# One-hot tiles of the expert gate matrix: a token's columns four bytes apart instead of sixteen

## The chip, the core and the metric

The kernel runs on one core of one Trainium2 chip. The metric is the device time of one execution in microseconds (us), the median of several runs. The engines have short names in the profile: PE is TensorE's matmul and PEld its weight load, DVE is VectorE, ACT is ScalarE, POOL is GpSimd and SP is SyncE, which here only issues DMAs.

## The reference, cut to what matters

The reference is three transformer blocks, one after the other, on 256 tokens of width 1024, in float32. The change lies in the last part of the first block, a layer of 16384 one-neuron experts. Each token has 8 heads. Each head scores 128 + 128 sub-keys, retrieves the 16 best pairs of them, and weighs the 16 experts that those pairs name by a softmax:

```python
v1, i1 = lax.top_k(s1, PEER_TOPK)            # s1, s2: scores of 128 sub-keys each
v2, i2 = lax.top_k(s2, PEER_TOPK)
cand = (v1[..., :, None] + v2[..., None, :]).reshape(T, PEER_HEADS, PEER_TOPK * PEER_TOPK)
cand_idx = (i1[..., :, None] * PEER_NKEYS + i2[..., None, :])...
vals, pos = lax.top_k(cand, PEER_TOPK)
experts = jnp.take_along_axis(cand_idx, pos, axis=-1)
gates = jax.nn.softmax(vals, axis=-1)
...
u = expert_u[ec]
a = jnp.einsum('cd,chkd->chk', xc, u)
w = jax.nn.gelu(a) * gc
return jnp.einsum('chk,chkd->cd', w, expert_v[ec])
```

So a token has 8 x 16 = 128 retrieved experts. Each is named by two numbers below 128, and each has a gate.

## The kernel before

The kernel does not gather experts. It multiplies every expert with every token, and weighs the products by a gate matrix that is zero where an expert was not retrieved. Three pieces of the class `Peer` matter here.

**The gate matrix** (the last loop of `routing`, lines 878 to 902). For one token the 128 x 128 matrix of gates is a product of two one-hot matrices: entry (b, a) is the sum, over the 128 retrieved experts on the partitions, of B[expert, b] times A[expert, a]. B has a one where b is the expert's second number. E has a one where a is its first number, and A is E times the gate. The gate goes in two float16 parts, so there are two tiles A, and each token takes two matmuls that accumulate in one float32 product. The loop makes 8 tokens in a step, and there are 32 steps. In each step DVE makes E (line 888), B (line 889) and the two A (line 892), each a float16 tile of 1024 elements per partition. PE then does 16 matmuls of 128 columns (line 897), each with its own weight load, into two PSUM tiles of four tokens. ACT copies each PSUM tile into `gt` (line 900), and after every second step it issues a DMA of `gt` to a scratch tensor `gd` in DRAM (line 902).

The tiles E, B and A are laid out as [128 partitions, 128 values, 8 tokens]. One token's 128 columns, which a matmul reads as `B[:, :, token]` and `A[j][:, :, token]`, thus stand eight float16 elements apart, which is 16 bytes. All four tiles come out of one pool of eight buffers (tag `oh`), so DVE can be about two steps ahead of PE. An A of a later step takes a buffer that the matmuls of an earlier step must have left.

**The up products** (`up`, lines 904 to 914). The experts' input weights stream through SBUF in 64 chunks of 1 MB. For each chunk ACT makes the high part `wh` (line 99), and for the first 29 chunks POOL, not DVE, makes the low part `wl = raw - wh` (line 101), in two halves each. PE multiplies the chunk with all tokens by 48 matmuls of 256 columns (lines 117 to 119, output `tp`), and ACT applies gelu (line 912) and leaves the result in a buffer `ga`.

**The order.** `run` weaves the two: `weave(self.routing(), up, n)` emits the steps of `routing`, and after some of them one chunk of `up`. Thirteen chunks come among the steps ahead of the gate loop, eleven more among the first of the 32 gate steps. A scheduler then spreads the matmuls of a chunk among the gate steps, and sets one fixed order for each engine, which the engine keeps. After the loop `down` (line 916) reads the gates back from `gd`, does the chunks that are left, and multiplies with the experts' output weights.

The constant `iota` (line 772) holds the numbers 0 to 127, each eight times. It is an operand of lines 888 and 889, and its first 16 values are an operand of line 859, ahead of the gate loop.

Of the kernel before, what the change touches and what calls it, by code (L numbers as in the profile page):

```python
# [26 lines left out]
class Core:  # L27
    """Pools and the pieces that every block uses.

    Weights stream through SBUF in chunks of [128, 2048]; each float32 chunk is split  # L30
    exactly into a part with 12 significant bits and the rest, and a float32 product is
    hi*hi + hi*lo + lo*hi, accumulated in float32.
    """
# [18 lines left out]
    def ring(self, ctx, n):  # L52
        """Buffers of the weight stream, n of the split parts."""
        self.raw = ctx.enter_context(self.tc.tile_pool(name="raw", bufs=3))
        self.slots, self.turn, self.early = [], 0, []
        self.more(ctx, n)

    def more(self, ctx, n):
        """n more buffers of the split parts while ctx is open."""
        pool = ctx.enter_context(self.tc.tile_pool(name=f"split{len(self.slots)}", bufs=n))  # L60
        self.slots += [pool] * n

        def less():
            del self.slots[-n:]
        ctx.callback(less)

    def work(self, ctx, half_rows=1):
        """Buffers of the norms: rows of gains, a token tile's rows."""
        self.row_bufs = {D: 3, 512: half_rows}
        self.wk = ctx.enter_context(self.tc.tile_pool(name="wk", bufs=1))  # L70

    def temp(self, ctx, name):
        """Buffers of one part of the kernel."""
        self.tmp = ctx.enter_context(self.tc.tile_pool(name=name, bufs=2))
        return self.tmp
# [45 lines left out]
    def row(self, name, n=D, src=None, pool=None, tag=None, p=128):  # L121
        """A row of a parameter on every partition."""
        src = self.a[name] if src is None else src
        t = (pool or self.wk).tile([128, n], F32, tag=tag or f"row{n}", name="row", bufs=1 if pool else self.row_bufs.get(n, 2))[:p]
        self.nc.scalar.dma_start(t, bass.AP(tensor=src.tensor, offset=src.offset, ap=[[0, p], [1, n]]))
        return t

    def rsqrt_n(self, ss, n, m, p=128):
        """(ss / n + EPS) ** -0.5 for [p, m]."""
        nc = self.nc  # L130
        v = self.sm.tile([128, 8], F32, tag="qv", name="qv")[:p, :m]
        y = self.sm.tile([128, 8], F32, tag="qy", name="qy")[:p, :m]
        nc.gpsimd.tensor_scalar(v, ss, 1.0 / n, EPS, op0=OP.mult, op1=OP.add)
        nc.gpsimd.tensor_tensor(y, v, self.half[:p, :m], op=OP.pow)
        return y

    def rstd(self, parts, n, p=128):
        """Reciprocal root mean square of rows of n that come in one or two parts [p, m <= 512]."""
# [17 lines left out]
    def pre_norm(self, t, g):  # L156
        """xh, xl[:, :, t] = split(transpose(rmsnorm(X[t]) * g))"""
# [10 lines left out]
    def put_off(self, f, *args):  # L168
        """Emits f(*args), now or at the next flush."""
# [10 lines left out]
    def post_norm(self, t, acc, g, scale, gn=None):  # L180
        """X[t] += scale * rmsnorm(acc) * g, and the next part's pre_norm if it has gains gn."""
# [10 lines left out]
    def residual(self, t, acc, gn):  # L192
        """X[t] += acc, and the next part's pre_norm."""
# [5 lines left out]
    def to_T(self, xn, hi, lo, t, nb, kb0=0, scale=None):  # L199
        """hi, lo[:, kb0.., t] = split(transpose(xn) * scale), scale a power of two."""  # L200
# [15 lines left out]
    def cols_steps(self, w, done):  # L216
        """w: [groups, 2, 128, 4 * N], N <= 512 output columns a group; done(j, t, psum).
        The first two groups go one token tile at a time, as the tiles get ready, if the ring has room."""
# [24 lines left out]
    def linear_stat(self, hl, i, ps):  # L243
        """ps [128, n] = 128 output features by tokens; hl: a chunk [128, 2, 8, 128], i: which half."""
# [5 lines left out]
    def lead(self, ch, done):  # L250
        """Products of the chunks ch one token tile at a time, as the tiles get ready, with the tokens as
        rows; done(c, t, psum [128, 2, 128])."""
# [9 lines left out]
    def pair(self, hl, between=lambda: None):  # L262
        """The two products of a chunk."""
# [6 lines left out]
    def stat_pairs(self, chunk, n, lead=0, row=None):  # L270
        """The two products of each of n chunks. The first chunks go one token tile at a time, with the
        tokens as rows [128, 256] in row(c, t), and are then transposed."""
# [30 lines left out]
    def linear_rows(self, w, hi, lo, done, tail=3, pool=0):  # L303
        """w: [K / 256, 128, 2048] rows in pairs of blocks; hi, lo: [128, K / 128, S]."""
# [34 lines left out]
def weave(main, side, n):  # L339
    """Emits the steps of main, and n[i] steps of side after step i."""  # L340
# [5 lines left out]
def head_norm(k, pool, ps, nh, gain, tag, p=128):  # L346
    """Per-head rmsnorm of ps [p, nh * 64]; returns [p, nh, 64] in SBUF."""
# [13 lines left out]
def rope(k, pool, q, nh, cs, sn, p=128):  # L361
    """Rotary embedding of the first 16 dims of q [p, nh, 64], in place; cs, sn: [p, 16]."""
# [10 lines left out]
def attend(k, pool, p, q, segs, v, identb, sink=None):  # L373
    """Masked attention of p queries and 8 heads.

    q(h): [64, p]; segs(h): (keys [64, n], n, additive mask [p, n] or None) for each piece of the
    keys; v(s, h): [n, 64]. Returns psum [p, 8, 64] before the division, and the factors [p, 8].
    """
# [65 lines left out]
def gelu_small(k, pool, out, x, n, p):  # L444
    """tanh form of gelu for small SBUF tiles, in the table of exp."""
# [10 lines left out]
class Block1:  # L456
# [108 lines left out]
    def compress(self):  # L565
        """The compressed keys and values; yields where the tensor engine would wait."""
# [59 lines left out]
    def cmp_scores(self, t):  # L626
        """Exponentials of the compressed keys' scores [128, 8, 15] and their factors [128, 8]."""
# [21 lines left out]
    def cmp_out(self, s):  # L649
        """psum [128, 8, 64]: the exponentials' products with the compressed values."""  # L650
# [12 lines left out]
    def attention(self, t):  # L663
# [10 lines left out]
        def add(b, o, r, first=False):  # L674
            """y = or += the gated output of branch b"""
# [20 lines left out]
    def flush(self, keep=0):  # L696
        """Emits the transposes that were put off, but for the last."""
# [3 lines left out]
    def merge(self):  # L701
        k, nc, pool = self.k, self.k.nc, self.pool
        M = [k.xn() for t in range(2)]
        for h in range(2):
            ch = [k.stream(k.a["w_up_" + n][h, 0]) for n in "ab"]
            for t in range(2):
                ts = slice(t * 128, t * 128 + 128)
                c = slice(h * 512, h * 512 + 512)
                for i, n in enumerate("ab"):
# [6 lines left out]
                    # sigmoid(z) = (1 + tanh(z / 2)) / 2; the half is in to_T  # L716
# [38 lines left out]
class Peer:  # L755
    """Every expert's product with every token; a gate matrix, zero where the expert was not
    retrieved, weighs them. The gates come from the top-k of the sub-keys' scores; as two float16 parts
    of SCALE times them they keep float32's 24 bits."""
# [10 lines left out]
    def consts(self):  # L769
        k = self.k  # L770
        tl = lambda n, sh, dt=F32: self.rp.tile(sh, dt, name=n)
        self.iota = tl("iota", [128, 128, 8], F16)
        k.nc.gpsimd.iota(self.iota, pattern=[[1, 128], [0, 8]], base=0, channel_multiplier=0,
# [17 lines left out]
    def routing(self):  # L791
# [21 lines left out]
        for t in range(2):  # L813
# [40 lines left out]
            for j in range(2):  # L854
# [5 lines left out]
                                        self.iota[:, 0:16, None, :].to_broadcast([128, 16, 16, 8]), op=OP.is_equal)  # L860
# [17 lines left out]
        for t in range(2):  # L878
            n = self.GRP
            for q in range(128 // n):  # L880
                c = slice(t * 128 + q * n, t * 128 + q * n + n)
                gt = pool.tile([128, 128, n], F32, tag="g8", name="gt", bufs=2)
                for w in range(n // 8):
                    c = slice(t * 128 + q * n + w * 8, t * 128 + q * n + w * 8 + 8)
                    oh = lambda n_: pool.tile([128, 128, 8], F16, tag="oh", name=n_, bufs=8)
                    B, E = oh("B"), oh("E")
                    bc = lambda x: x[:, None, c].to_broadcast([128, 128, 8])
                    nc.vector.tensor_tensor(E, bc(self.iT[0]), self.iota, op=OP.is_equal)
                    nc.vector.tensor_tensor(B, bc(self.iT[1]), self.iota, op=OP.is_equal)
# [3 lines left out]
                    for z in range(2):  # L893
                        ps = k.tp(tag="tp")
                        for i in range(4):
                            for j in range(2):
                                nc.tensor.matmul(ps[:, i, :], B[:, :, z * 4 + i], A[j][:, :, z * 4 + i],
# [86 lines left out]
class Block2:  # L984
    def __init__(self, k, wc):
        """wc: pool of the block's constants."""
# [22 lines left out]
    def ffn(self, l, f, gn):  # L1009
        k, nc = self.k, self.k.nc  # L1010
        with ExitStack() as ctx:
# [6 lines left out]
            def hidden(x, n):  # L1018
                """The gated rows or columns of the products x [128, 2, n]."""
# [26 lines left out]
    def conv(self):  # L1046
        k, nc, a = self.k, self.k.nc, self.k.a
        with ExitStack() as ctx:
# [11 lines left out]
            # the taps: blocks 0..4 on the vector engine, 5 on ACT and GpSimd, 6 and 7 as products with diagonals,  # L1060
            # and so the first of block 4's
# [15 lines left out]
            def advance(n):  # L1077
                """n steps of the vector engine's blocks, in turn."""
# [79 lines left out]
    def hgrn(self):  # L1158
        k, nc, a = self.k, self.k.nc, self.k.a
        with ExitStack() as ctx:  # L1160
# [11 lines left out]
            # q, F and kk of a group of four heads; V and SG, two tiles each, follow them in their memory  # L1172
# [130 lines left out]
class Block3:  # L1303
    """Two layers over 16 meta tokens and the 256 tokens. The meta tokens follow the others in the
    transposed tiles; as stationary operand their hi and lo parts go side by side (rows 0 and 32 up)."""
# [47 lines left out]
    def meta_cols(self, mt, xx, k0, k1):  # L1353
        """The meta tokens' columns of blocks k0.. of xx [128, 2, n, SM]: hi, then lo 32 columns on."""
# [3 lines left out]
    def meta_mm(self, ps, mt, kb, wh, wl, start, stop):  # L1358
        """ps [64, n]: rows 0.. hi's products, rows 32.. lo's; their sum is the product."""
# [4 lines left out]
    def meta_sum(self, ps, n):  # L1364
        """[16, n] in SBUF from rows 0.. and 32.. of ps."""
# [17 lines left out]
    def qkv(self, l, pool, nt):  # L1383
        """Queries, keys and values of the layer."""
# [7 lines left out]
        def flush(keep=0):  # L1392
            """Emits the transposes that were put off, but for the last."""
# [41 lines left out]
    def attention(self, l, t, sink, g):  # L1435
        """Attention of token tile t, normalised, into yy[:, :, 0:4]."""
# [21 lines left out]
    def conv(self, l, nt):  # L1458
        """The gated convolution: yy[:, :, 4:8] = split(y * g), and the rows' rstd of y."""
# [55 lines left out]
    def out_part(self, chunks, operand, nt, done, before=lambda i: None):  # L1515
        """Products with chunks of rows (rows, c); operand(c): their pair of blocks, hi and lo [128, 2, 2, n]
        and the meta tokens' tile; done(t, [psum, psum]); before(i) emits what comes before chunk i."""
# [82 lines left out]
    def mlp(self, l, nt):  # L1600
        k, nc, a = self.k, self.k.nc, self.k.a
        with ExitStack() as ctx:
# [10 lines left out]
            def up(c):  # L1613
                """Blocks 2c and 2c + 1 of the hidden features."""
# [27 lines left out]
            def rows(c, t, p):  # L1642
                """The hidden rows of token tile t."""
# [58 lines left out]
def layout(i):  # L1702
    """The arrays of the launch: the inputs in the order in which the core reads them."""
# [107 lines left out]
```

## Time and profile before

| what | us |
|---|---|
| median of 3 runs | 3044.96 |
| the 3 runs | 3044.13 to 3054.55 |
| the profiled execution, first to last instruction (span) | 3048.1 |
| PE busy in the span | 2919.3 |
| gate loop, first to last matmul of line 897 and the step's end | 463.7 to 682.8 |
| the same as a length | 219.1 |

The page gives the profiled execution's own time as its span. It is 3.1 us (0.1%) over the median of the runs.

A row of a group of instructions reads: line, engine, operation, output <- inputs, shape, count, then the busy time of the group, the mean duration of one in ns, and the engine's idle time just before them with what ended it. A row of the timeline reads: start, duration, engine, line, operation, output <- inputs, shape, count, and in brackets the idle time before it and what ended that. A row of a table by windows gives for each engine its busy time and, in brackets, its instructions, and then the granted clock of TensorE as a share of full speed. A matmul's duration in these rows has its latency in it, so that durations of neighbours overlap. How fast matmuls follow each other is read from their starts.

### The profile page before, as it was taken

The page shows a single profiled execution, that of the slowest core. Times are in us where ns is not written, and L with a number is a line of the kernel's source. Part 1 is how long each engine was busy: PE and PEld are TensorE (multiplying, and loading weights), DVE is VectorE, ACT ScalarE, POOL GpSimd, SP SyncE. Part 2 cuts the span into 40 slices and gives each one's busy share as a digit, 9 for nine tenths or more (in the row PEclk, how much of TensorE's full clock was granted, in tenths as well). Part 3 has the DMA queues.
Part 4 walks back from the last instruction along what each step waited for, and adds up shares of the span by engine and source line. Part 5 has one row for each costly group of instructions (what it writes and reads, how often), then busy time and mean ns, then how long its engine had stood idle before and what let it go on. Part 6 is the DMA issues. An engine that isn't in the chain of part 4 may idle for free. (4 is left out here: it accounts for less than half of the span.)

```text
span 3048.1 us, 44684 instructions
## 1 busy us (share of the span) xinstructions
PE 2919.3 (96%) x18182; PEld 2586.9 (85%) x18182; DVE 1773.9 (58%) x2984; ACT 1367.2 (45%) x2318; POOL 421.3 (14%) x337
## 2 busy tenths in 40 slices
PE   8999979999999999999679999999999989999999
PEld 6787978889999988898669989898997878878897
DVE  6645693437555555655966555476655555455654
ACT  4533433335444555544535444343544444444543
POOL 2000663221000000000650000032001010000100
PEclk9968988789999999999889999999999899998999
DMA  5512433339766555554325555543554424443453
GB/s 211 187 56 85 153 124 130 134 137 324 251 205 211 206 193 193 205 187 169 131 69 182 185 194 181 192 156 116 175 182 153 145 87 166 152 139 111 145 187 111
DMA packets 105982, 496.74 MB, mean 163 GB/s; under 512 B 11040, under 2 KB 44320, under 8 KB 50224
## 3 DMA queue, kind: packets, MB, share of 16 engines
q1 hardware_dynamic: 61632, 443.15, 42.1%
q10 hardware_dynamic: 44144, 50.74, 5.0%
q8 instruction: 142, 2.33, 0.3%
q14 instruction: 64, 0.52, 0.1%
HBM read 476.03 MB, written 17.83 MB: 162 GB/s over the span
## 5 line engine op out<-in xcount | busy, mean ns | idle before, releaser
L101 DVE TENSOR_TENSOR wl<-raw,wh 128x1024 fp32r<-128x1024 f32 x764 | 915.4, 1219 | 617.7 <-ACT wh L99 616.4
L99 ACT CAST wh<-raw 128x1024 fp32r<-128x1024 f32 x848 | 861.3, 1041 | 708.2 <-PE acc L118 220.5
L117 PE MATMUL tp<-xx,wh 128*128 128x256 f32 (+1 forms) x1440 | 424.2, 295 | 5.6 <-ACT ga L912 5.6
L119 PE MATMUL acc<-xx,wl 128*128 128x256 f32 x1504 | 425.1, 283 | 2.2 <-POOL wl L101 1.4
L117 PE MATMUL acc<-xx,wh 128*128 128x256 f32 x1504 | 424.6, 282 | 2.4 <-DVE hp L1093 2.4
L118 PE MATMUL acc<-xx,wh 128*128 128x256 f32 x1504 | 425.5, 283 | 0.0
L118 PE MATMUL tp<-xx,wh 128*128 128x256 f32 (+1 forms) x1440 | 421.8, 293 | 0.0
L119 PE MATMUL tp<-xx,wl 128*128 128x256 f32 (+1 forms) x1440 | 420.6, 292 | 0.8 <-POOL wl L101 0.8
L117 PEld LDWEIGHTS tp<-xx,wh 128*128 128x128 f32 x1440 | 286.7, 199 | 10.5 <-ACT ga L912 6.0
L118 PEld LDWEIGHTS tp<-xx,wh 128*128 128x128 f32 x1440 | 287.1, 199 | 3.7
L119 PEld LDWEIGHTS acc<-xx,wl 128*128 128x128 f32 x1504 | 286.9, 191 | 2.6 <-POOL wl L101 1.6
L117 PEld LDWEIGHTS acc<-xx,wh 128*128 128x128 f32 x1504 | 286.6, 191 | 2.6 <-issue 2.6
L119 PEld LDWEIGHTS tp<-xx,wl 128*128 128x128 f32 x1440 | 286.4, 199 | 1.8 <-POOL wl L101 1.0
L118 PEld LDWEIGHTS acc<-xx,wh 128*128 128x128 f32 x1504 | 284.7, 189 | 0.0
L147 POOL TENSOR_SCALAR va<-ss 128x1 f32<-128x1 f32 (+1 forms) x49 | 26.0, 531 | 1810.3 <-ACT junk L143 1628.8
L101 POOL TENSOR_TENSOR wl<-raw,wh 128x1024 fp32r<-128x1024 f32 x84 | 219.5, 2630 | 232.8 <-ACT wh L99 221.3
L117 PE MATMUL acc<-wh,xx 128*128 128x256 f32 (+2 forms) x672 | 223.3, 334 | 3.2 <-ACT xx L112 3.2
L118 PE MATMUL acc<-wl,xx 128*128 128x256 f32 (+2 forms) x672 | 219.7, 328 | 4.2 <-DVE wl L101 4.2
L119 PE MATMUL acc<-wh,xx 128*128 128x256 f32 (+2 forms) x672 | 218.7, 328 | 1.2 <-DVE xx L113 1.2
L928 PE MATMUL o<-wh,wth 128*128 128x512 f32 x512 | 200.6, 392 | 0.0
L929 PE MATMUL o<-wl,wth 128*128 128x512 f32 x512 | 200.1, 391 | 0.0
L931 PE MATMUL o<-wh,wtl 128*128 128x512 f32 x512 | 159.9, 391 | 0.0
(480 smaller groups left out, 5113.2 us busy)
## 6 DMA issues: line engine op xcount, KB each, us to landing
raw<-in_ffn_in_dram SPq DMA_DIRECT2D x88, 1024.0 KB, 4.9
raw<-in_peer_u_dram SPq DMA_DIRECT2D x64, 1024.0 KB, 4.9
raw<-in_peer_v_dram SPq DMA_DIRECT2D x64, 1024.0 KB, 4.9
raw<-in_ffn_out_dram SPq DMA_DIRECT2D x44, 1024.0 KB, 4.9
raw<-in_w_up_dram SPq DMA_DIRECT2D x32, 1024.0 KB, 4.9
raw<-in_w_down_dram SPq DMA_DIRECT2D x32, 1024.0 KB, 4.9
gd<-gt ACTq DMA_DIRECT2D x16, 1024.0 KB, 4.0
G<-gd ACTq DMA_DIRECT2D x16, 1024.0 KB, 7.0
```

The source lines that it names most:

```text
L99: nc.scalar.copy(h[:, c], r[:, c])
L101: eng.tensor_tensor(l[:, c], r[:, c], h[:, c].bitcast(F32), op=OP.subtract)
L117: mm(out, ah, bh, start=start, stop=False)
L118: mm(out, ah, bl, start=False, stop=False)
L119: mm(out, al, bh, start=False, stop=stop)
L147: nc.gpsimd.tensor_scalar(v, ss[:, 0:1], EPS, ss[:, 1:2], op0=OP.add, op1=OP.add)
L928: mm(acc[t][h], wh, vh[:, h], start=st, stop=False)
L929: mm(acc[t][h], wh, vl[:, h], start=False, stop=False)
L931: mm(acc[t][h], wl, vh[:, h], start=False, stop=sp)
```

## The change

The three kinds of one-hot tiles get the layout [128 partitions, 4 pairs of tokens, 128 values, 2 tokens]. One token's 128 columns now stand two float16 elements apart, which is four bytes, within a run of 512 bytes that a pair of tokens shares. DVE's four operations in a step keep their count, their 1024 elements per partition and their type. Their patterns differ: the operand that holds the tokens' numbers or gates is now read in rows of two elements, each row 128 times over, where it was one row of eight elements, 128 times over. The output stays one unbroken run.

The numbers 0 to 127 now stand twice each in a constant of its own, `iota2`, which is read four times over in an operation. `iota` shrinks to the 16 values that line 859 (now 862) needs.

```diff
-        self.iota = tl("iota", [128, 128, 8], F16)
-        k.nc.gpsimd.iota(self.iota, pattern=[[1, 128], [0, 8]], base=0, channel_multiplier=0,
+        self.iota = tl("iota", [128, 16, 8], F16)
+        k.nc.gpsimd.iota(self.iota, pattern=[[1, 16], [0, 8]], base=0, channel_multiplier=0,
+                         allow_small_or_imprecise_dtypes=True)
+        self.iota2 = tl("iota2", [128, 128, 2], F16)
+        k.nc.gpsimd.iota(self.iota2, pattern=[[1, 128], [0, 2]], base=0, channel_multiplier=0,
                          allow_small_or_imprecise_dtypes=True)
...
-                                        self.iota[:, 0:16, None, :].to_broadcast([128, 16, 16, 8]), op=OP.is_equal)
+                                        self.iota[:, :, None, :].to_broadcast([128, 16, 16, 8]), op=OP.is_equal)
...
-                    oh = lambda n_: pool.tile([128, 128, 8], F16, tag="oh", name=n_, bufs=8)
+                    oh = lambda n_: pool.tile([128, 4, 128, 2], F16, tag="oh", name=n_, bufs=8)
                     B, E = oh("B"), oh("E")
-                    bc = lambda x: x[:, None, c].to_broadcast([128, 128, 8])
-                    nc.vector.tensor_tensor(E, bc(self.iT[0]), self.iota, op=OP.is_equal)
-                    nc.vector.tensor_tensor(B, bc(self.iT[1]), self.iota, op=OP.is_equal)
+                    bc = lambda x: x[:, c].rearrange("p (a b) -> p a b", b=2)[:, :, None].to_broadcast([128, 4, 128, 2])
+                    iota = self.iota2[:, None].to_broadcast([128, 4, 128, 2])
+                    nc.vector.tensor_tensor(E, bc(self.iT[0]), iota, op=OP.is_equal)
+                    nc.vector.tensor_tensor(B, bc(self.iT[1]), iota, op=OP.is_equal)
                     A = [oh(f"A{j}") for j in range(2)]
                     for j in range(2):
                         nc.vector.tensor_tensor(A[j], E, bc(self.gT[j]), op=OP.mult)
...
-                                nc.tensor.matmul(ps[:, i, :], B[:, :, z * 4 + i], A[j][:, :, z * 4 + i],
+                                nc.tensor.matmul(ps[:, i, :], B[:, z * 2 + i // 2, :, i % 2], A[j][:, z * 2 + i // 2, :, i % 2],
                                                  start=j == 0, stop=j == 1)
```

On PE, DVE, ACT and SP the instructions stand in the same order as before. On POOL one instruction is added, where the experts' part begins. The rows show the difference there, with `hss`, `qv`, `va` and `ya` being small tiles of norms:

```order
 L134 TENSOR_TENSOR qy<-qv,half 15x2
-L773 IOTA iota 128x1024
+L773 IOTA iota 128x128
+L776 IOTA iota_2385 128x256
 L147 TENSOR_SCALAR va<-ss 128x1
 L150 TENSOR_TENSOR ya<-va,half 128x1
```

One fill of 1024 elements per partition becomes two, of 128 and of 256 elements, at the same place.

## The prediction

> **What bounds the kernel now.** I read the page first, then one table by windows over the gate loop, then its groups, its waits and its timeline. The page says whose kernel this is:
>
> ```profile
> span 3048.1 us, 44684 instructions
> ...
> PE 2919.3 (96%) x18182; PEld 2586.9 (85%) x18182; DVE 1773.9 (58%) x2984; ACT 1367.2 (45%) x2318; POOL 421.3 (14%) x337
> ```
>
> PE is busy for 96% of the span. The change touches one stage, so that stage alone decides. The table by windows gives the gate loop, and inside it a stretch at half clock:
>
> ```profile
> core 0: us, PE busy (x) PEld busy (x) DVE busy (x) ACT busy (x) POOL busy (x), PEclk, DMA share, GB/s
> 463.70:682.80 219.10, 219.10 (x1148) 176.07 (x1148) 81.42 (x119) 70.48 (x114) 62.90 (x25) 0.82 0.35 130
> 516.40:526.60 10.20, 10.20 (x48) 8.77 (x47) 5.00 (x8) 3.11 (x5) 2.91 (x1) 0.50 0.59 207
> ```
>
> PE has no gap in 219.1 us, DVE is busy for 81 of them, POOL for 63, ACT for 70, and the granted clock averages 0.82. The groups of the same window say what PE does, and what DVE and POOL do:
>
> ```profile
> L897 PE MATMUL tp<-A,B 128*128 128x128 f16 x512 | 126.5, 415 | 0.0
> L117 PE MATMUL tp<-xx,wh 128*128 128x256 f32 x212 | 73.4, 346 | 0.0
> L118 PE MATMUL tp<-xx,wh 128*128 128x256 f32 x212 | 72.9, 344 | 0.0
> L119 PE MATMUL tp<-xx,wl 128*128 128x256 f32 x212 | 71.8, 339 | 0.0
> ...
> L101 POOL TENSOR_TENSOR wl<-raw,wh 128x1024 fp32r<-128x1024 f32 x25 | 65.0, 2601 | 155.4 <-ACT wh L99 144.2 <-PE tp L897 11.3
> ...
> L892 DVE TENSOR_TENSOR A<-E,gT 128x1024 f16<-128x1024 f16 x60 | 43.8, 770 | 124.1 <-PE tp L897 124.1
> ...
> L889 DVE TENSOR_TENSOR B<-iT,iota 128x1024 f16<-128x1024 f16 x29 | 22.1, 763 | 2.1 <-PE tp L897 2.1
> L888 DVE TENSOR_TENSOR E<-iT,iota 128x1024 f16<-128x1024 f16 x29 | 19.8, 683 | 0.0
> ```
>
> 512 gate matmuls share the stage with 3 x 212 = 636 up matmuls. DVE does 60 + 29 + 29 = 118 operations there, and waits 124 us in all, always for the gate matmuls. So PE sets the pace, and DVE waits for buffers that PE is slow to leave.
>
> How slow is read from starts in the timeline, here of one gate step and the up matmuls behind it:
>
> ```profile
> 463.76 3.93 PE L897 MATMUL tp<-A,B 128*128 128x128 f16 x16
> ...
> 467.32 0.48 PE L117 MATMUL tp<-xx,wh 128*128 128x256 f32 x1
> ...
> 467.64 0.28 PE L118 MATMUL tp<-xx,wh 128*128 128x256 f32 x1
> ...
> 468.11 0.28 PE L119 MATMUL tp<-xx,wl 128*128 128x256 f32 x1
> ```
>
> Sixteen gate matmuls take 467.32 - 463.76 = 3.56 us, 0.223 us each for 128 columns. Four up matmuls, from the one at 467.64 to the one at 468.11, take 0.47 us, 0.117 each for 256 columns. Half the columns take twice the time. Per byte of a partition's row that is passed over they agree: 128 columns 16 bytes apart are 2048 bytes in 0.223 us, 9.2 bytes per ns; 256 float32 columns are 1024 bytes in 0.117 us, 8.8 bytes per ns. I read this as one limit, the rate at which the moving operand's row is passed over.
>
> **The change, part by part: the matmuls.** At four bytes apart, 128 columns span 512 bytes. At 8.8 bytes per ns that is 0.0585 us, so 512 of them take 30.0 us instead of 512 x 0.223 = 114.2. The weight loads, 16 bytes apart too, are behind the matmuls now; they stay there if they follow as the up matmuls' do, one 128-column load in each 0.117 us or faster. At that bound the 512 take 59.9 us. I take 0.0585, since the byte rates of the two rows agree, and keep 0.117 as the other end.
>
> The Trainium skill, page "TensorE: Matmul & The Clock Gate", section "Back-to-back issue gap", gives about 81 ns for each matmul of 128 columns in a stream where each has its own weight load. By it the 512 take an estimated 41.5 us. No run here shows that stream yet.
>
> The up matmuls: 636 x 0.117 = 74.4 us at full clock. Before, 219.1 - 114.2 = 104.9 us went to them, 30 more, and this is the clock. At half clock they start 0.215 us apart:
>
> ```profile
> 522.10 0.42 PE L117 MATMUL tp<-xx,wh 128*128 128x256 f32 x1
> 522.32 0.42 PE L118 MATMUL tp<-xx,wh 128*128 128x256 f32 x1
> 522.53 0.41 PE L119 MATMUL tp<-xx,wl 128*128 128x256 f32 x1
> ```
>
> The clock falls in this stage while PE shows no gap, in stretches full of gate steps: slow columns seem to count as little work. With dense gate matmuls I expect most of the 30 us back. PE's sum is then 30.0 + 74.4 = 104 us (134 at the slower end).
>
> **DVE and POOL, which are late next.** DVE's operations, and POOL's halves of `wl` (line 101), in three places:
>
> ```profile
> 476.93 1.29 DVE L892 TENSOR_TENSOR A<-E,gT 128x1024 f16<-128x1024 f16 x2 [6.94 <-PE tp L897]
> 478.14 0.69 DVE L888 TENSOR_TENSOR E<-iT,iota 128x1024 f16<-128x1024 f16 x1
> 478.74 0.69 DVE L889 TENSOR_TENSOR B<-iT,iota 128x1024 f16<-128x1024 f16 x1
> ...
> 478.77 2.91 POOL L101 TENSOR_TENSOR wl<-raw,wh 128x1024 fp32r<-128x1024 f32 x1 [1.93 <-ACT wh L99]
> ...
> 548.61 2.87 DVE L889 TENSOR_TENSOR B<-iT,iota 128x1024 f16<-128x1024 f16 x1
> ...
> 548.52 2.41 POOL L101 TENSOR_TENSOR wl<-raw,wh 128x1024 fp32r<-128x1024 f32 x1 [1.58 <-ACT wh L99]
> ...
> 446.74 6.57 POOL L101 TENSOR_TENSOR wl<-raw,wh 128x1024 fp32r<-128x1024 f32 x1 [2.60 <-ACT wh L99]
> ```
>
> Undisturbed, DVE starts one every 0.60 us ((478.74 - 476.93) / 3), and POOL takes 2.41. Where they meet, one waits the other out: DVE's 0.69 became 2.87 beside a POOL operation that had just begun, and POOL's 2.41 became 2.91 behind DVE's last operation, and 6.57 beside a row of them. So their times add up: 118 x 0.60 + 25 x 2.41 = 70.8 + 60.3 = 131 us, above PE's 104. This pair, not PE, should be the stage's next bound.
>
> That bound holds if nothing is lost at hand-overs, and something is. A's buffers still come free by PE's steps, POOL's halves start behind ACT's casts, which stand in ACT's queue behind copies of `ps` that wait for PE, and the up matmuls wait for POOL. I add a tenth, 13 us, which is also what the window's own busy times say with their waits for each other in them: 81.4 + 62.9 = 144.3. I take 144 us for the stage. Ends: 104 (PE alone, if the pair overlaps more than these rows show) and 175, where a third is lost at hand-overs.
>
> ACT's 70 us of work in the window are unchanged and fit in 144.
>
> The `iota` split costs nothing that counts. POOL's fill stands alone:
>
> ```profile
> 281.18 1.94 POOL L773 IOTA iota<- 128x1024 f16 x1 [157.41 <-DVE xn L722]
> 296.70 0.30 POOL L147 TENSOR_SCALAR va<-ss 128x1 f32<-128x1 f32 x1 [13.58 <-ACT junk L143]
> ```
>
> POOL idles 13.6 us after it, and the next operation waits for ACT. Were that cover gone, the two fills, 384 elements in place of 1024, would at most double its 1.94 us.
>
> **The sum.** 219.1 - 144 = 75 us come off. Outside the stage nothing moves, so all of it reaches the end: behind the loop PE goes straight on with the up matmuls. The profiled span, 3048.1 us, is 3 us above the median of the runs shown; I take the 75 from the median, 3044.96 - 75 = 2970 us. By the stage's ends it is 2930 (104) to 3001 (175).
>
> **Rivals.**
>
> *DVE loses its double rate (chance 0.09).* All four operations now read an operand in rows of two elements. That they run two elements a tick is read from these rows of line 888 and of a float32 line:
>
> ```profile
> L888 DVE TENSOR_TENSOR E<-iT,iota x32: 678/684/687, 420.8 to 663.5; 128x1024 f16<-128x1024 f16 x32
> ...
> L101 DVE TENSOR_TENSOR wl<-raw,wh 128x1024 fp32r<-128x1024 f32 x764 | 915.4, 1219 | 617.7 <-ACT wh L99 616.4
> ```
>
> 1024 float16 elements take 0.684 us, 1024 float32 elements 1.219. At the lower rate each operation is 0.535 us longer, 118 of them 63 us: 131 + 63 + 13 = 207, and the time is 3033; without hand-over losses 3020. For it: no row here shows such an operand at the double rate. Against it: the output stays one run, and line 1209 reads float32 rows of 1, 2, 4 and up to 64 elements by the code, nearly all at one price:
>
> ```profile
> L1209 DVE TENSOR_TENSOR qq<-q,F x16: 679/693/1139, 2022.1 to 2095.3; 128x512 f32<-128x512 f32 x16
> ```
>
> The Trainium skill, page "Vector Engine (DVE) Microarchitecture Reference", section "Performance modes — why throughput varies by op and dtype", reports that the vendor's rule denies the double rate to two elements per partition, and that the chip was measured to grant it. [...]
>
> *DVE pays for each short row (0.04): slower than before.* If each row of two costs a tick more on top of the single rate, an operation has 1536 ticks where it has 512. A tick is 0.535 / 512 = 1.045 ns, so each operation is 1.07 us longer, 118 of them 126 us. The stage becomes 131 + 126 = 257 us, 38 more than now, and the time 3083. It decides from (219 - 131) / 118 = 0.75 us more per operation, 1.43 us each. Line 1209 speaks against it.
>
> *The clock stays low (0.05).* With DVE and POOL as the bound PE has gaps, and the clock may fall for most of the stage. At half clock the up matmuls take 636 x 0.215 = 137 us, with 30 for the gates 167, with a tenth lost 183: 36 us come off, 3009. Against it: the loop's first 18.6 us hold two gate steps and most of a third beside up matmuls, at full clock, and the new mix has more columns in each us:
>
> ```profile
> 463.70:482.30 18.60, 18.60 (x112) 14.58 (x112) 6.20 (x11) 8.48 (x13) 10.89 (x5) 1.00 0.46 170
> ```
>
> *The matmuls do not get faster (0.03).* If 0.223 us belongs to something other than the distance of the columns, such as the weight load that goes with each, the time stays at 3045. The equal byte rates speak against it.
>
> **How the numbers follow.** The forecast has 0.79. A measurement of this kernel can tell about 0.5%, 15 us, from no change, so faster begins below 3029.7. Faster: 0.79, the clock's 0.05, and two thirds of the first rival, 0.06: 0.90. Same: the rest of that rival, 0.03, and the last, 0.03: 0.06. Slower: 0.04. The range runs from 2935, near PE's own bound, to 3015, which takes in the forecast's bad end and the clock's rival, and leaves out some 0.16.
>
> **What would show it right or wrong.** Right: gate steps of 16 matmuls within about 1 us; DVE's four operations still 0.68 us each; PE with gaps in the stage that end on DVE's A or POOL's `wl`; the stage near 144 us, and the clock near 1. Wrong: DVE operations of 1.2 us or more; gate steps still of 3.5 us; a stage without gaps at half clock; or a stage near 104, which would say that DVE and POOL do not add up.

## The result, and the profile after

The changed kernel takes 2957.95 us, the median of 4 runs (2956.89 to 2960.15), where the kernel before takes 3046.05 (4 runs, among them the three that were shown). The ratio is 0.9705, with a 95% interval of 0.9688 to 0.9721. That is 88 us less, in the range of the prediction and 12 us below its number.

The tables by windows over the gate loop (here 468.1 to 596.5 us) and the page's first line answer to those of before. The columns are the window, its length, then busy time and instructions of PE, PEld, DVE, ACT and POOL, then clock, DMA share and GB/s:

```profile
span 2958.5 us, 44682 instructions
```

```profile
468.10:596.50 128.40, 113.95 (x1149) 110.49 (x1147) 119.23 (x119) 65.49 (x114) 78.98 (x25) 0.95 0.60 222
```

The loop fell from 219.1 to 128.4 us. PE now has 14 us of gaps in it. DVE and POOL together show 198 us of busy time in 128, so much of it must be waiting for each other. The clock's mean rose from 0.82 to 0.95.

The spans balance: 3048.1 - 2958.5 = 89.6 us. The loop gave 90.7 of them. It began 4.4 us later than before, and from its end to the last instruction there are 3.3 us less.

PE's timeline shows one gate step between up matmuls:

```profile
481.54 0.28 PE L117 MATMUL tp<-xx,wh 128*128 128x256 f32 x1
481.67 1.09 PE L902 MATMUL tp<-A,B 128*128 128x128 f16 x16
482.56 0.36 PE L118 MATMUL tp<-xx,wh 128*128 128x256 f32 x1
```

Sixteen gate matmuls take 482.56 - 481.67 = 0.89 us, 0.056 each, where they took 0.223. Lines 893 and 897 (888 and 892 before) say what became of DVE's operations. Each row has the shortest, the median and the longest of a line in ns:

```profile
L893 DVE TENSOR_TENSOR E<-iT,iota x32: 675/678/2879, 420.6 to 589.7; 128x1024 f16<-128x1024 f16 x32
```

```profile
L897 DVE TENSOR_TENSOR A<-E,gT x64: 675/679/2899, 448.0 to 591.5; 128x1024 f16<-128x1024 f16 x64
```

The median is 0.68 us as before: rows of two elements cost DVE nothing. The longest are those that met a POOL operation. How the two engines take turns is seen in the timelines of DVE and POOL between 486 and 495 us:

```profile
486.44 0.68 DVE L893 TENSOR_TENSOR E<-iT,iota 128x1024 f16<-128x1024 f16 x1
487.04 0.68 DVE L894 TENSOR_TENSOR B<-iT,iota 128x1024 f16<-128x1024 f16 x1
487.65 1.28 DVE L897 TENSOR_TENSOR A<-E,gT 128x1024 f16<-128x1024 f16 x2
...
492.80 2.55 DVE L897 TENSOR_TENSOR A<-E,gT 128x1024 f16<-128x1024 f16 x1 [0.26 <-PE tp L902]
```

```profile
486.86 7.93 POOL L101 TENSOR_TENSOR wl<-raw,wh 128x1024 fp32r<-128x1024 f32 x1 [5.11 <-ACT wh L99]
```

POOL's half of `wl`, 2.4 us of work, was issued at 486.86, while DVE had a row of operations to do without a wait. It ended at 494.79, after DVE's first pause at 492.5. DVE's next operation then waited for it in turn and took 2.55 us. The waits within the loop name the engine that is late now:

```profile
POOL wl L101 <- ACT wh L99: 49.4, 11, 8.4
...
ACT gt L905 <- PE tp L902: 29.1, 18, 5.1
PE tp L902 <- DVE A L897: 12.7, 10, 4.8
PEld L902 <- DVE A L897: 9.9, 4, 5.0
...
DVE A L897 <- PE tp L902: 4.9, 6, 1.8
...
PEld tp L119 <- POOL wl L101: 1.9, 1, 1.9
```

DVE waited 124 us for the gate matmuls. Now it waits 4.9, and the gate matmuls and their weight loads wait for DVE. The up matmuls wait for POOL's `wl` itself hardly at all, 1.9 us. POOL's waits for ACT are idle time of an engine that had nothing given to it yet.

### The profile page after: what moved, and what is told of

It is laid out like the page before. It is cut to its first block, busy times and chain, and to the rows that moved or that the text cites. A ratio compares the mean times of both kernels' runs of the same rounds, so it can differ in the third digit from the quotient of the medians.

```text
span 2958.5 us, 44682 instructions
## 1 busy us (share of the span) xinstructions
PE 2811.3 (95%) x18182; PEld 2519.8 (85%) x18182; DVE 1813.7 (61%) x2984; ACT 1362.9 (46%) x2318; POOL 433.4 (15%) x338
## 5 line engine op out<-in xcount | busy, mean ns | idle before, releaser
L117 PE MATMUL tp<-xx,wh 128*128 128x256 f32 (+1 forms) x1440 | 413.2, 287 | 5.7 <-ACT ga L917 5.7
L119 PE MATMUL tp<-xx,wl 128*128 128x256 f32 (+1 forms) x1440 | 410.9, 285 | 2.5 <-POOL wl L101 2.5
L118 PE MATMUL tp<-xx,wh 128*128 128x256 f32 (+1 forms) x1440 | 411.0, 285 | 0.0
L117 PEld LDWEIGHTS tp<-xx,wh 128*128 128x128 f32 x1440 | 276.6, 192 | 9.1 <-ACT ga L917 6.1
L118 PEld LDWEIGHTS tp<-xx,wh 128*128 128x128 f32 x1440 | 276.8, 192 | 2.4
L119 PEld LDWEIGHTS tp<-xx,wl 128*128 128x128 f32 x1440 | 276.2, 192 | 3.0 <-POOL wl L101 2.9
L101 POOL TENSOR_TENSOR wl<-raw,wh 128x1024 fp32r<-128x1024 f32 x84 | 231.6, 2779 | 133.0 <-ACT wh L99 132.8
```

What stands on the lines that cost most here:

```text
L101: eng.tensor_tensor(l[:, c], r[:, c], h[:, c].bitcast(F32), op=OP.subtract)
L117: mm(out, ah, bh, start=start, stop=False)
L118: mm(out, ah, bl, start=False, stop=False)
L119: mm(out, al, bh, start=False, stop=stop)
```

## The experiments

Two theories were to be told apart in two places. What made the gate matmul slow: the moving operand's distance or the weight load's, and what in that distance? And what bounds the loop now: DVE and POOL, which shut each other out, or PE with the waits in its own chain?

| kernel | columns apart (moving / stationary) | 16 gate matmuls, us | loop, us | clock in it | time, us |
|---|---|---|---|---|---|
| before | 16 / 16 bytes | 3.56 | 219.1 | 0.82 | 3046.05 |
| changed | 4 / 4 | 0.89 | 128.4 | 0.95 | 2957.95 |
| e1, `wl` by DVE | 4 / 4 | 0.90 | 108.1 | 1.00 | 2943.06 |
| e2, moving alone | 4 / 16 | 1.03 | 129.1 | 0.96 | 2954.97 |
| e3, stationary alone | 16 / 4 | 3.46 | 220.0 | 0.79 | 3049.91 |
| e4 | 8 / 8 | 1.81 | 135.5 | 1.00 | 2967.52 |
| e5 | 2 / 2 | 0.87 | 198.4 | 0.86 | 3032.1 |
| e6, before with `wl` by DVE | 16 / 16 | 3.57 | 221.8 | 0.78 | 3052.34 |
| e7, changed once more | 4 / 4 | 0.91 | 127.1 | 0.96 | 2950.79 |
| e8 | 32 / 4 | 3.52 | not comparable | | 3061.4 |

The times of e1 and e6 are medians of 4 and 10 runs; of e2 to e5, e7 and e8 there is one run each, so that some us between them say nothing. Beside e1 to e4 the kernel before ran at 3049.1 us, beside e5 to e8, on another chip, at 3051.0. Some results lie just outside the range that was expected: e2 3.0 us below, e5 2.1 and e6 0.3 us above, and the clock of e3 at 0.79 instead of 0.80 or more. Each is far from what its rival called for.

**e1: `wl` of the loop's chunks made by DVE.**

```diff
-            hl = k.stream(k.a["peer_u"][c], pool=c < self.AHEAD // 2)
+            hl = k.stream(k.a["peer_u"][c], pool=c < 13)
```

> The changed kernel, with the low parts wl of the eleven or so chunks that lie in the gate loop made by DVE instead of POOL. The first theory says that DVE and POOL, whose operations shut each other out, bound the changed gate loop at 128 us: their sum falls from 118 x 0.60 + 25 x 2.41 = 131 us to 118 x 0.60 + 25 x 1.13 = 99 us, below PE's 104 to 108, so the loop takes 108 to 115 us and the kernel 2938 to 2946 us. The rival says that PE with the waits in its own chain (buffers, copies of PSUM) bounds the loop: then DVE, which gets 28 us more of work, lets nothing go faster, and the kernel stays at 2958 us or gets slower.

Measured: 2943.06 us, ratio to before 0.9661 (0.9642 to 0.9680), below the 0.9705 of the changed kernel. The loop by windows:

```profile
464.20:572.30 108.10, 105.46 (x1127) 103.35 (x1126) 98.21 (x141) 64.14 (x112) 0.00 (x0) 1.00 0.71 260
```

DVE does more work than in the changed kernel, and the loop is 20 us shorter. So DVE and POOL as a pair were the bound, and with POOL out of the loop PE, busy for 105.5 us of 108.1, is the bound again. PE's sum was worked out as 104. Part of the 20 us is the clock's: PE's gaps fell from 14.4 to 2.6 us, and its busy time, at full clock throughout, from 114.0 to 105.5. How much of it reaches the end is less sure. The time is 15 us below the changed kernel's median, but only 8 below its run in e7, and neither was measured beside e1.

**e2 and e3: one operand in pairs.** In e2 the stationary tile B keeps the old layout and an `iota8` like the old constant; in e3 A and E do.

```diff
+                    oh8 = lambda n_: pool.tile([128, 128, 8], F16, tag="oh", name=n_, bufs=8)
+                    bc8 = lambda x: x[:, None, c].to_broadcast([128, 128, 8])
-                    B, E = oh("B"), oh("E")
+                    B, E = oh8("B"), oh("E")
...
-                                nc.tensor.matmul(ps[:, i, :], B[:, z * 2 + i // 2, :, i % 2], A[j][:, z * 2 + i // 2, :, i % 2],
+                                nc.tensor.matmul(ps[:, i, :], B[:, :, z * 4 + i], A[j][:, z * 2 + i // 2, :, i % 2],
```

```diff
-                    B, E = oh("B"), oh("E")
+                    B, E = oh("B"), oh8("E")
...
-                    A = [oh(f"A{j}") for j in range(2)]
+                    A = [oh8(f"A{j}") for j in range(2)]
...
-                                nc.tensor.matmul(ps[:, i, :], B[:, z * 2 + i // 2, :, i % 2], A[j][:, z * 2 + i // 2, :, i % 2],
+                                nc.tensor.matmul(ps[:, i, :], B[:, z * 2 + i // 2, :, i % 2], A[j][:, :, z * 4 + i],
```

> The changed kernel, with the stationary tile B back in the layout of before (16 bytes apart) and only the moving tiles A, with E, in pairs. If the moving operand's row sets the rate, gate matmuls follow each other every 0.057 us as in the changed kernel, or at most as fast as weight loads from 16 bytes apart allow, some 0.065 to 0.12, and the kernel takes 2958 to 2970 us. If the weight load's distance set the rate, they stay at 0.223 us and the kernel at 3045.

> The changed kernel, with the moving tiles A and with them E back in the layout of before (16 bytes apart) and only the stationary tile B in pairs. If the moving operand's row sets the rate, gate matmuls stay at 0.22 to 0.23 us, PE shows no gap in the gate loop, the clock falls in it to a mean of 0.8 to 0.85, and the kernel takes 3040 to 3050 us. If the weight load's distance set the rate, the kernel takes 2958.

Measured: e2 2954.97 us, e3 3049.91. The step of each kernel, first e2, then e3:

```profile
462.56 1.23 PE L907 MATMUL tp<-A,B 128*128 128x128 f16 x16
463.59 0.36 PE L117 MATMUL tp<-xx,wh 128*128 128x256 f32 x1
```

```profile
462.74 3.82 PE L907 MATMUL tp<-A,B 128*128 128x128 f16 x16
466.20 0.54 PE L117 MATMUL tp<-xx,wh 128*128 128x256 f32 x1
```

The moving operand carries nearly all of it: 1.03 us a step with it alone in pairs, 3.46 with the weights alone. Weights from 16 bytes apart cost some 0.008 us a matmul, 4 us in all on PE, which DVE and POOL's bound hides. e3 also shows what the slow columns do to the clock: with the moving columns 16 bytes apart the clock's mean in the loop is 0.79, and with only that undone (the changed kernel) 0.95. In e3 PE shows no gap that could account for it:

```profile
462.70:682.70 220.00, 220.00 (x1147) 166.28 (x1146) 83.91 (x119) 70.22 (x114) 63.60 (x25) 0.79 0.35 129
```

**e4: eight bytes apart.**

```diff
-                    oh = lambda n_: pool.tile([128, 4, 128, 2], F16, tag="oh", name=n_, bufs=8)
+                    oh = lambda n_: pool.tile([128, 2, 128, 4], F16, tag="oh", name=n_, bufs=8)
```

The constant, the broadcasts and the matmul's indices follow.

> The changed kernel with tokens in fours instead of pairs: a token's columns stand eight bytes apart. By the rate at which bytes of a row are passed over, 8.8 to 9.2 per ns, a gate matmul passes over 1024 bytes and takes 0.111 to 0.117 us; PE's sum is 512 x 0.114 + 75 = 133 us, about as much as DVE and POOL's, and the kernel takes 2960 to 2985 us. The rival is that a second column on the same 16 bytes is all that full rate needs: the gate matmul stays at 0.057 us and the kernel at 2958. This rival is the Trainium skill's rule, page SBUF - State Buffer, section Specifications (TRN2): lines of 16 bytes that need two or more hits each for full bandwidth.

Measured: 2967.52 us.

```profile
463.78 2.06 PE L902 MATMUL tp<-A,B 128*128 128x128 f16 x16
465.59 0.37 PE L117 MATMUL tp<-xx,wh 128*128 128x256 f32 x1
```

```profile
463.80:599.30 135.50, 135.50 (x1149) 133.20 (x1147) 115.94 (x119) 69.26 (x114) 63.61 (x25) 1.00 0.56 210
```

1.81 us a step, 0.113 a matmul, twice the price of four bytes. PE has no gap in 135.5 us, and its sum was given as 133. The Trainium skill, page "SBUF — State Buffer", section "Specifications (TRN2)", says that 16-byte lines need two or more hits each for full bandwidth. Here two columns in 16 bytes run at half the rate of four, so for a matmul's moving operand at full clock the measurement decides: two are not enough. The loop, though, lost only 7 us against the changed kernel, because PE's sum came just above that of DVE and POOL.

**e8: 32 bytes apart,** with half of each tile unused. Only the distance between matmuls is read here, since fewer chunks lie in the loop (434 up matmuls where the kernel before has 636; that is nine chunks' worth, not the three that were expected).

```diff
-    AHEAD = 58
+    AHEAD = 42
...
-                    oh8 = lambda n_: pool.tile([128, 128, 8], F16, tag="oh", name=n_, bufs=8)
+                    oh8 = lambda n_: pool.tile([128, 128, 16], F16, tag="oh", name=n_, bufs=8)[:, :, 0:8]
```

(The last two lines are against e3.)

> The kernel with only the stationary tile in pairs, and the moving tiles 32 bytes apart: tiles A and E of 16 token places of which 8 are used. For room in SBUF only 42 buffers of up products are kept instead of 58, so that three chunks instead of eleven lie in the gate loop and the kernel's time is not comparable; what is read is the distance between gate matmuls. If the cost is the bytes passed over, they follow each other every 0.45 us. If each column that starts new 16 bytes costs the same however far it jumps, they stay at 0.22 to 0.23 us.

Measured, one step and the matmul behind it:

```profile
463.21 3.89 PE L907 MATMUL tp<-A,B 128*128 128x128 f16 x16
466.73 0.48 PE L117 MATMUL tp<-xx,wh 128*128 128x256 f32 x1
```

3.52 us, as at 16 bytes. Bytes passed over are not the cost, since twice as many of them cost the same.

**e5: two bytes apart,** one token alone in its run.

```diff
-                    oh = lambda n_: pool.tile([128, 4, 128, 2], F16, tag="oh", name=n_, bufs=8)
+                    oh = lambda n_: pool.tile([128, 8, 128], F16, tag="oh", name=n_, bufs=8)
...
-                    bc = lambda x: x[:, c].rearrange("p (a b) -> p a b", b=2)[:, :, None].to_broadcast([128, 4, 128, 2])
+                    bc = lambda x: x[:, c][:, :, None].to_broadcast([128, 8, 128])
```

> The changed kernel with one token alone in its run: its columns stand two bytes apart, side by side. DVE's operands with the tokens' numbers are then read in rows of one element, each 128 times. By the rate of bytes passed over a gate matmul would need 0.03 us, but no column rate above that of the up matmuls (0.117 us for 256) has been seen, so it stays at 0.057. If rows of one element cost DVE its double rate, its operations take 1.2 us in place of 0.68, DVE and POOL sum to 118 x 1.13 + 25 x 2.41 = 194 us, and the kernel takes 3015 to 3030 us. If they do not, it stays at 2955 to 2960.

Measured: 3032.1 us, and DVE's line 897:

```profile
L897 DVE TENSOR_TENSOR A<-E,gT x64: 1209/1214/3439, 439.3 to 662.8; 128x1024 f16<-128x1024 f16 x64
```

```profile
467.10:665.50 198.40, 142.84 (x1286) 136.25 (x1284) 182.89 (x121) 77.63 (x130) 125.21 (x29) 0.86 0.44 159
```

The matmuls are as fast as at four bytes (0.87 us a step), and DVE's operations take 1.21 us in place of 0.68. That takes back most of the gain. This is what the first rival of the prediction feared: one element to a row costs the double rate, two do not. The loop holds four more POOL operations here than assumed: 118 x 1.13 + 29 x 2.41 = 203 us, and 198.4 were measured.

**e6: e1's edit in the kernel before.**

> The kernel before, 16 bytes apart, with wl of the gate loop's chunks made by DVE instead of POOL, as in the first experiment. If DVE and POOL bound only the changed kernel, and PE the one before, this gives nothing here: 3040 to 3052 us. If moving wl to DVE is a gain of its own, the 15 us show here as well: 3030 us or less.

Measured: 3052.34 us, ratio 1.0011 (0.9998 to 1.0024). Taking POOL out of the loop is worth nothing while PE, at 16 bytes, has no gap:

```profile
455.10:676.90 221.80, 221.66 (x1128) 178.46 (x1127) 100.15 (x141) 69.12 (x112) 0.00 (x0) 0.78 0.34 128
```

**e7: the changed kernel once more.**

> The changed kernel once more, unchanged. Its gate loop started at 468.1 us, where that of the kernel before and of four others started between 462.6 and 464.2. If this belongs to the program, the loop starts near 468 again and the time is 2956 to 2960 us; if it is chance in the order in which DVE and POOL meet ahead of the loop, it starts anywhere from 462 to 469, and the time goes with it.

Measured: 2950.79 us, and the loop from 462.3 on, not from 468:

```profile
462.30:589.40 127.10, 112.64 (x1149) 109.12 (x1147) 119.28 (x119) 65.48 (x114) 78.27 (x25) 0.96 0.61 224
```

So the late start in the first profile is not the program's: the same kernel started 5.8 us earlier here. In the first profile POOL's halves between 430 and 455 us stand in twos, the first at 430.95, where e7 has five in a row from 427.22. What tips it was not tried, and one run does not tell whether it differs from run to run or from chip to chip. Measured against the 3051.0 beside it, this run is 100 us below the kernel before, where the four of the result were 88.

## Why the prediction was right, point by point

**The matmuls.** Forecast 0.0585 us each, with 0.117 as the other end; measured 0.056 to 0.057. The size was right, the reading behind it was not, and that part is luck. The prediction took the bytes passed over as one limit for gate and up matmuls alike, since their rates agreed (9.2 and 8.8 bytes per ns). e8 refutes it: 32 bytes apart cost as much as 16. The clock refutes it too. In the kernel before, the stretch from 516.40 to 526.60 ran at half clock, and there up matmuls start 0.215 us apart instead of 0.117. A gate step in the same stretch reads:

```profile
518.15 3.94 PE L897 MATMUL tp<-A,B 128*128 128x128 f16 x16
521.73 0.57 PE L119 MATMUL tp<-xx,wl 128*128 128x256 f32 x1
```

That is 3.58 us, and 3.56 at full clock. So the up matmul follows the clock and the gate matmul 16 bytes apart does not: two limits, whose rates happen to be alike at full clock. Four bytes apart, the gate matmul does follow it, as the changed kernel's longest stretch at half clock shows:

```profile
523.00:529.80 6.80, 4.36 (x27) 4.11 (x28) 6.80 (x9) 1.20 (x2) 1.53 (x1) 0.50 0.90 352
```

```profile
525.13 0.29 PE L902 MATMUL tp<-A,B 128*128 128x128 f16 x1 [4.77 <-DVE A L897]
...
527.61 1.08 PE L902 MATMUL tp<-A,B 128*128 128x128 f16 x8
528.45 0.56 PE L119 MATMUL tp<-xx,wl 128*128 128x256 f32 x1
```

Eight take 0.84 us, 0.105 each instead of 0.056. At four bytes it thus runs at the up matmuls' rate per column: half of their columns in half of their 0.117 us, which is the forecast's 0.0585 for another reason.

Farther apart, the runs fit one price for each 16 bytes of a row from which a column is taken. 128 columns touch 16-byte pieces 128 times at 16 and at 32 bytes (0.22), 64 times at eight bytes (0.113): some 1.75 us for 1000 pieces in each. By this price the 32 pieces at four bytes would take 0.056 as well, so at full clock the two limits cannot be told apart there. At two bytes, with 16 pieces, it stays at 0.054, as the rate per column has it.

The Trainium skill, page "TensorE: Matmul & The Clock Gate", section "Back-to-back issue gap", gives 81 ns for a matmul of 128 columns in a stream with a weight load for each. Here each had its own, and 56 to 57 ns were measured, so the measurement decides.

**The clock.** Expected to come back with dense gate matmuls, and it did in the main: 0.82 to 0.95, and 1.00 in e1 and e4, where PE has few gaps or none. That the slow columns bring the half clock with them is shown by e3. They are not alone in it: e5's gate matmuls are as fast as the changed kernel's, and its clock averaged 0.86, with PE idle for 55.6 us of 198.4. In the changed kernel the stretch from 523.0 to 529.8 begins within PE's longest gap, the 4.77 us before 525.13. So the prediction's rival of a low clock came true in small part, and its 30 us for the gates at half clock were too few: at 0.105 us each they are 54.

**DVE and POOL as the next bound.** Right in kind: e1 shows it from one side, e6 shows that it did not hold before. The sum of 131 us was some 8 too high. With the rows of both engines laid over each other, at least one of them was busy for 122.8 us of the loop. Two of the 25 halves of `wl` lie mostly outside it (they start at 465.97 and 595.82), and where the engines take turns they overlap a little:

```profile
476.02 5.74 POOL L101 TENSOR_TENSOR wl<-raw,wh 128x1024 fp32r<-128x1024 f32 x2 [1.07 <-ACT wh L99]
```

```profile
476.02 3.48 DVE L897 TENSOR_TENSOR A<-E,gT 128x1024 f16<-128x1024 f16 x2
479.42 2.88 DVE L893 TENSOR_TENSOR E<-iT,iota 128x1024 f16<-128x1024 f16 x1
482.23 0.68 DVE L894 TENSOR_TENSOR B<-iT,iota 128x1024 f16<-128x1024 f16 x1
```

From 476.02 to 482.23 three DVE operations and two halves took 6.21 us, where the sum gives 3 x 0.60 + 2 x 2.41 = 6.62.

**The hand-overs: the term that was mis-sized.** A tenth, 13 us, was added to 131, and the stage was to take 144. Measured were 128.4 and 127.1 us. Something was lost, but less: DVE stood idle for 9.2 us of 128.4, 4.9 of them in waits for the gate matmuls and 4.3 behind its last operation, which ended at 592.2. POOL worked through some of this, so that both were idle for only 5.6 us. That the loop fell below the bare sum is thus no sign of a perfect hand-over; the sum was too high by more than the loss. The window's busy sum of 144, which the text took as a sign for the tenth, counts the waits of the two for each other as busy time, so it says nothing about idle time. The loop came out 15.6 us below 144 and the time 12 below 2970; the later start of the loop took some of it back.

**DVE's double rate.** Kept at rows of two elements (0.68 us), as forecast. e5 shows that the risk was real one step further on. What the Trainium skill, page "Vector Engine (DVE) Microarchitecture Reference", section "Performance modes — why throughput varies by op and dtype", says of two elements per partition is about operations of that size. The ones here have 1024 per partition, in rows of two, so that the runs neither bear it out nor contradict it.

**The constants.** POOL's fills took 0.36 and 1.53 us in place of 1.94, far from anything that waits.

```profile
L773 POOL IOTA iota<- x1: 361/361/361, 280.9 to 280.9; 128x128 f16 x1
```

```profile
L776 POOL IOTA iota<- x1: 1525/1525/1525, 281.2 to 281.2; 128x256 f16 x1
```

## What to carry to other kernels

When a matmul takes longer than its column count says, look at how far apart its moving columns stand before looking at weights or waits: at full clock, four columns in each 16 bytes ran here at full rate, two at half, one at a quarter. Two rates that agree at one clock need not be one limit; compare them where the clock is lower. Choose the layout by both ends: the run that suits the matmul (two bytes apart) cost the engine that writes it its double rate, and pairs served both. Then add up the times of engines that shut each other out, DVE and POOL here, because their sum is the next bound; moving one engine's share to the other, worth nothing before the change, took 20 us off the loop after it, of which 8 to 15 reached the end.

## What was not expected of the hardware

A moving operand does not pay for the distance beyond 16 bytes: 3.52 us a step at 32 bytes, 3.56 and 3.46 at 16. At 16 bytes it does not pay for the clock either: 3.58 us at half clock. The weight load pays far less than the moving operand for the same distance: 0.064 us a matmul with weights 16 bytes apart, 0.056 with four. POOL can be held off by a row of DVE operations for long: one half of `wl`, 2.4 us of work, took 7.93 us, for as long as DVE's operations followed one another without a pause. Where they had once met, the two took turns: DVE's operations at 516.68 and 519.48 took 2.88 and 2.85 us, each beside one half. And PE without a gap in the profile can run at half clock for 10 us at a time, as from 516.40 to 526.60 in the kernel before.
